# Where the operands of w_out begin in SBUF, and idle products around the second small turn, in a gated short-convolution layer on one Trainium2 core

## The chip, the cores and the metric

The kernel runs on one core of a Trainium2 chip. The metric is the device time of one execution in microseconds. The time before is the median of three runs, 915.63 us (915.52 to 916.85). One more execution was profiled; the rows quoted below are of that one.

## The reference

One layer is run (DEPTH is 1, so the recurrent mixer of the reference is never reached). Everything is float32.

```python
h = rmsnorm(x, norm_g)                                  # x: 256 tokens x 2048
shift, scale, gate = split(silu(c) @ ada_w + ada_b, 3)  # ada_w: 2048 x 6144
h = h * (1 + scale) + shift
b, cg, v, g = split(h @ w_in, 4)                        # w_in: 2048 x 16384
u = causal_conv3(cg * v)                                # per channel, 4096 channels
y = b * u * silu(g)                                     # 256 x 4096
x = x + gate * (y @ w_out)                              # w_out: 4096 x 2048
return rmsnorm(x, final_g)
```

## The kernel before

A float32 product is made of three products of a faster type: each operand is cast to `fp32r` ("hi"), the rest that the cast lost is the second operand ("lo"), and hi*hi, hi*lo and lo*hi are summed in PSUM. In the profile these are matmuls of 128 rows by 128 columns of weights with 256 or 512 columns of the moving operand.

**The order of the work.** The first some 26 us (lines 179 to 390) prepare. ScalarE's queue loads `rows1` (c, norm_g, ada_b), SyncE's queue loads x, the first slices of ada_w (`at0`) and of w_in. TensorE turns 16 rows of `rows1` for silu(c) ("the first small turn", line 243), turns the other 64 rows into `tp_v` ("the second small turn", line 246), and then makes `IDLE` = 6 idle products (`idle`, line 236), whose results nobody reads: a 128 x 128 float32 weight `ident` against a broadcast column of `ones`, 512 columns, each of them two records in the profile. Then x is turned, four 128-wide slices at a time (`turn_x`, line 284), with the sums of ada_w for shift and scale between (`sum0`, line 355: TensorE takes the slices k in `ON_PE`, VectorE the others at lines 377 and 379, and a product with `ones` adds VectorE's part, line 381). The order of this part is written out by hand: `in_order()` pins each engine's instructions to the order of the text.

Up to about 381 us the first half of w_in runs (`mm_s`, `part`, line 476) in an order that `plan()` makes, because shift and scale arrive piece by piece; then the second half up to about 731 us (`mm_b`, line 605). In both the slices of w_in are the stationary operand, 128 columns at a time, and the turned tokens `hT` are the moving operand, 256 columns (tokens) (`product`, line 447). From 731 us w_out runs, in four column blocks `dc` of 512 (line 771). Here it is the other way round: y (the layer's middle result, 128 tokens) is stationary, and hi or lo of a slice of w_out, 512 columns, is moving (`out_mm`, line 659). In blocks 0 and 1 the slices `ep` 5, 6 and 7, in block 2 the slices 5 and 6, are done by `seven` (line 689), a Strassen-like scheme on products of 256 columns: 42 products for each slice, whose stationary operands are y or sums of y (`form`, `form_g`, `form_h`). The slices come in the order 0, 1, 2, 5, 3, 6, 4, 7. Where nothing is pinned, a simulating scheduler sets the order within each engine.

**Buffers.** Each slice of weights is loaded into `raw` (SyncE's queue), ScalarE casts it to `hi` (line 321), VectorE subtracts to `lo` (line 326). All three kinds are 8 KB per partition and come from one pool, `wpool`, with three buffers each for the tags `raw`, `hi` and `lo`. In w_out the roles of two tags are exchanged: the slice is loaded into the tag `lo`, and the lo part goes to the tag `raw`. In the last block each loaded slice is first multiplied by the gate (line 796). A buffer is used again when its last reader is done, so a cast to `hi` waits for the products that read that buffer three slices before, and a load waits for VectorE.

**Where the buffers begin.** A pool puts its tiles one behind the other. Small unused tiles (`line`, `line0`, `line2`, `line3`, `line4`) shift what follows them. As the pools of this kernel lay the tiles out, these are the first bytes modulo 256 of what the products read:

| operand | in w_in | in w_out, before | in w_out, changed |
| --- | --- | --- | --- |
| moving | hT: 0 | hi and lo: 64 | hi and lo: 0 |
| stationary | hi: 64, lo: 192 | y, form, form_g: 128; form_h: 0 | y, form, form_g: 64; form_h: 0 |

Every slice that a product takes from such a tile is a multiple of 256 bytes further, so that all products of one row of the table have the same remainder.

Of the kernel before, what the change touches and what calls it, by code (L numbers as in the profile page):

```python
# [13 lines left out]
P = 128  # L14
# [103 lines left out]
def short_conv_layer(ctx: ExitStack, tc: tile.TileContext, x, c, norm_g, ada_w, ada_b, w_in, conv_w, w_out, final_g, out):  # L118
# [5 lines left out]
    line = ctx.enter_context(tc.tile_pool(name="line", bufs=1, side="right"))  # L124
    line.tile([P, 56], F32, tag="line", name="line")
    const = ctx.enter_context(tc.tile_pool(name="const", bufs=1))
    const.tile([P, 32], F32, tag="line0", name="line0")
    adap = ctx.enter_context(tc.tile_pool(name="adap", bufs=2))
    wpool = ctx.enter_context(tc.tile_pool(name="wpool", bufs=2))
    psum = ctx.enter_context(tc.tile_pool(name="psum", bufs=3, space=PSUM))  # L130
    hpool = ctx.enter_context(tc.tile_pool(name="hpool", bufs=1, side="right"))
    line2 = ctx.enter_context(tc.tile_pool(name="line2", bufs=1, side="right"))
    line2.tile([P, 32], F32, tag="line2", name="line2")
    slots = ctx.enter_context(tc.tile_pool(name="slots", bufs=NSLOT, side="right"))

    def slot(shape, name, dtype=F32):
        return slots.tile(shape, dtype, tag="slot", name=name)

    def raw_tile(name):
        return wpool.tile([P, SLOT], F32, tag="raw", name=name, bufs=3)  # L140

    after = mybir.DependencyInfo(mybir.DependencyClass.NoSync, mybir.DependencyReason.DATA)

# [37 lines left out]
    pinned.enter_context(in_order())  # L181


    rows1 = const.tile([80, P], F32, tag="rows1", name="rows1")
    rows2 = const.tile([96, P], F32, tag="rows2", name="rows2")
    HX = D // 2
    GIVE = 300
    LEAD = 80
    IDLE = 6
    ON_PE = (3, 7, 10, 11, 13, 15)  # L190
    xt = [[slot([P, HX], f"x{t}{dh}") for dh in range(2)] for t in range(TT)]
    nc.scalar.dma_start(rows1[64:80, :], c.rearrange("o (k p) -> (o k) p", p=P))
# [8 lines left out]
    adas = ada_w[0].rearrange("(k p) (s f) -> p k s f", p=P, s=3)  # L201
    NK0 = ADA[0]
    first_ada = []
    wpool.tile([P, 16], F32, tag="line4", name="line4", bufs=1)
    for n, (j, kk) in enumerate(((0, 4), (4, 4), (8, 4), (12, 2), (14, 1), (15, 1))):
        at = wpool.tile([P, SLOT], F32, tag=("lo", "hi")[n % 2], name="at0", bufs=3)[:, : kk * 2 * NK0 * P]
        at = at.rearrange("p (k s f) -> p k s f", k=kk, s=2)
        if n == 0:
            wpool.tile([P, 32], F32, tag="line3", name="line3", bufs=1)
        for s in range(2):  # L210
            nc.sync.dma_start(at[:, :, s, :], adas[:, j : j + kk, s, 0 : NK0 * P])
        first_ada.extend(at[:, i] for i in range(kk))
# [3 lines left out]

    ident = const.tile([P, P], F32, tag="ident", name="ident")
    make_identity(nc, ident)
    ones = const.tile([P, P], F32, tag="ones", name="ones")
    nc.vector.memset(ones, 1.0)  # L220
    eps_t = const.tile([P, 1], F32, tag="eps", name="eps_t")
    nc.vector.memset(eps_t, EPS)
# [5 lines left out]
    def turn(rows, lo, n, dst):  # L228
        tp = psum.tile([P, 512], F32, tag="sm", name="tp_v", bufs=2)[:, : n - lo]
        nc.tensor.transpose(tp, rows[lo:n, :], ident[lo:n, lo:n])  # L230
        if dst is not None:
            nc.vector.tensor_copy(dst, tp)
        return tp


    def idle(n):
        for _ in range(n):
            nc.tensor.matmul(tp_idle, ident, ones[:, 0:1].to_broadcast([P, 512]), start=True, stop=True)  # L238
# [4 lines left out]
    silu = nc.scalar.activation(silu_c, turn(rows1, 64, 80, None), AF.Silu)  # L243
    root = nc.scalar.activation(warm, eps_t, AF.Sqrt)
    tc.add_manual_dep(root.ins, silu.ins.name, after, reason="one change of table")
    tp_v = turn(rows1, 0, 64, None)
    gT = vec[:, 0:KT]
    bias = vec[:, KT : 3 * KT].rearrange("p (s k) -> p s k", s=2)
    idle(IDLE)


    ssq = const.tile([P, 2, TT], F32, tag="ssq", name="ssq")
# [57 lines left out]
            )  # L310
            nc.vector.tensor_tensor(out=hl_[k], in0=hf, in1=hh_[k].bitcast(F32), op=ALU.subtract)

    def hi_tile():
        return wpool.tile([P, SLOT], F32R, tag="hi", name="hi", bufs=3)

    def lo_tile(lo_tag="lo"):
        return wpool.tile([P, SLOT], F32R, tag=lo_tag, name="lo", bufs=3)

    def split_hi(raw, n, hi=None):
        hi = hi_tile() if hi is None else hi  # L320
# [17 lines left out]
        other_half[0] = tiles if n <= HALF else None  # L338
        return tiles

    def split(raw, n, lo_tag="lo"):

        return split_lo(raw, n, split_hi(raw, n), lo_tag)

# [174 lines left out]
    for kind, *step in plan():  # L521
        if kind == "ada":
            ada_piece(*step)
        else:
            ch, k1 = step[0], step[3]
            part(*step)
            if step[2] == 0 and len(acc) in LATER:
                with tc.issue_after(last_mm[0].ins), behind(ended):
                    if len(acc) == LATER[0]:
                        nc.sync.dma_start(rows2[:, :], conv_w.rearrange("w (k p) -> (w k) p", p=P))  # L530
                    else:
                        turn(rows2, 0, 96, cw)
            whole[ch] += k1 == KT
            if k1 == KT and whole[ch] == 4:
                mixed(ch)
# [26 lines left out]
    def gate_sums(dc, j, at3):  # L562
        nc.sync.dma_start(at3, adas[:, j : j + 2, 2, dc * 512 : (dc + 1) * 512])
        if j == 0:
            gacc[0] = adap.tile([P, 512], F32, tag="gv", name="gacc")
        ga = gacc[0]
        for i in range(2):
            s = silu_c[:, j + i : j + i + 1]
            if j + i == 0:
                nc.vector.tensor_scalar_mul(ga, at3[:, i, :], s)  # L570
            else:
                nc.vector.scalar_tensor_tensor(out=ga, in0=at3[:, i, :], scalar=s, in1=ga, op0=ALU.mult, op1=ALU.add)  # L572
        if j + 2 == KT:
            ps = psum.tile([P, 512], F32, tag="sm", name="ps_gate", bufs=2)
            nc.tensor.matmul(ps, ones, ga, start=True, stop=True)  # L575
            nc.vector.tensor_tensor(out=gate(dc), in0=ps, in1=gate(dc), op=ALU.add)

    KP = 8
# [110 lines left out]
    def seven(po, ps, ep, raw):  # L689


        opens = ep == SEVEN[0]
        if opens:
            first_of.clear()
        b = blocks(raw)
        sums = wpool.tile([P, SLOT], F32, tag="lo", name="sums_o", bufs=3)
        s = blocks(sums)
        nc.vector.tensor_tensor(
            out=s[:, :, 0:2], in0=b[:, :, 1:3], in1=b[:, :, 0:1].to_broadcast([P, 2, 2, NB]), op=ALU.subtract
        )  # L700
        hi, lo = hi_tile(), lo_tile("raw")
        bh, bl = blocks(hi), blocks(lo)
        nc.scalar.copy(bh[:, :, 1:4], b[:, :, 1:4])
        nc.vector.tensor_tensor(out=s[:, :, 2], in0=b[:, :, 2], in1=s[:, :, 0], op=ALU.add)
        nc.vector.tensor_tensor(out=s[:, :, 3], in0=b[:, :, 3], in1=s[:, :, 2], op=ALU.subtract)
        nc.vector.tensor_tensor(out=bl[:, :, 1:4], in0=b[:, :, 1:4], in1=bh[:, :, 1:4].bitcast(F32), op=ALU.subtract)
        sh, sl = (blocks(v) for v in split(sums, SLOT, "raw"))

        def y(pair, k, t):
            return [ys[pair][:, k, h, t * P : (t + 1) * P] for h in range(2)]  # L710

        def f(pair, j):
            return [forms[pair][h][:, j] for h in range(2)]

        left, right = slice(0, NB), slice(NB, 2 * NB)
        for r in range(2):
            pair = ep * 2 + r
            for dst, bank, form, j in (
                (ps[:, 1, left], 1, y(pair, 0, 0), 1),
                (po[0][:, right], None, y(pair, 1, 0), 3),  # L720
                (po[0][:, left], None, f(pair, 3), 2),
            ):
                seven_mm(dst, bank, opens and r == 0 and bank is not None, form, bh[:, r, j], bl[:, r, j])
        for r in range(2):
            pair = ep * 2 + r
            for dst, bank, form, j in (
                (ps[:, 0, left], 0, f(pair, 2), 1),
                (ps[:, 0, right], 0, f(pair, 0), 0),
                (ps[:, 1, right], 1, f(pair, 1), 2),
                (po[1][:, right], None, y(pair, 1, 1), 3),  # L730
            ):
                seven_mm(dst, bank, opens and r == 0 and bank is not None, form, sh[:, r, j], sl[:, r, j])
# [38 lines left out]
    for dc in range(4):  # L771
# [13 lines left out]
        for ep in orders[dc]:  # L785

            first = dc == 0 and ep == 0
            raw = wpool.tile([P, SLOT], F32, tag="raw" if first else "lo", name="raw_o", bufs=3)
            nc.sync.dma_start(
                raw.rearrange("p (k f) -> p k f", k=EP),  # L790
                w_out[0, ep * EP * P : (ep + 1) * EP * P, dcs].rearrange("(k p) f -> p k f", p=P),
            )
            if dc == 3:

                raw3 = raw.rearrange("p (k f) -> p k f", k=EP)
                nc.vector.tensor_tensor(  # L796
                    out=raw3, in0=raw3, in1=gate(dc).unsqueeze(1).to_broadcast([P, EP, 512]), op=ALU.mult
                )
            if dc == 0:
                load_ends(orders[dc].index(ep) - 3)  # L800
            if ep in sevens[dc]:
                seven(po, ps, ep, raw)
                continue
            hi, lo = split(raw, SLOT, "raw")
            out_mm(po[0], 0, ep, hi, lo)
            if dc == 3 and ep >= n_ep - LATE:
                late.append((ep, hi, lo))
            else:
                out_mm(po[1], 1, ep, hi, lo)
# [52 lines left out]
```

## Time and profile before

| | |
| --- | --- |
| median of three runs | 915.63 us |
| the profiled execution: its time, its span | 916.7 us, 914.6 us |
| preparation, up to the first product of w_in | 0 to 26.5 us |
| w_in, first half (`mm_s`), second half (`mm_b`) | 26.5 to 381 us, 381 to 731 us |
| w_out: first product, last product begins | 730.9 us, 905 us |
| busy in 731 to 848 us: TensorE, VectorE, ScalarE | 116.99, 94.61, 57.67 us of 117 |

The rows are read like this. A row of the timeline has the start in us, the busy time in us, the engine, the line, the operation, what is written <- what is read, the shapes, the count of merged instructions, and in brackets how long the engine was idle before and what ended that. "PE" is TensorE's matmul, "PEld" its load of a stationary operand, which overlaps matmuls; "DVE" is VectorE, "ACT" ScalarE, "SP" SyncE, which issues most DMAs. The duration of one matmul has its latency in it, and consecutive ones overlap: the pace is read from start to start. A row of the chain of waits has start, length, and what the end of the program hung on in that time, with the count of instructions.

### The profile page before, as it was taken

To read this page: it belongs to the slowest core of one execution; us is meant where nothing else is said; L and a number is where in the kernel's file an instruction comes from. 1 tells how busy PE (TensorE), PEld (TensorE's weight loads), DVE (VectorE), ACT (ScalarE), POOL (GpSimd) and SP (SyncE) were. 2 spreads that over 40 slices of the span, in tenths; PEclk is the share of its full clock that TensorE was granted. 3 is DMA by queue.
4 is the path that set the end of the run, shared out by engine and by line. 5 is a ranking of instruction groups with operands and counts; after the bars stand their busy time and mean duration, and the time that the engine had idled before them with its cause. 6 is when DMAs were issued, how large, how long until landed. Compare 5 with 4: busy or idle time off the path is not lost.

```text
span 914.6 us, 16626 instructions
## 1 busy us (share of the span) xinstructions
PE 897.3 (98%) x7191; PEld 862.6 (94%) x7191; DVE 665.3 (73%) x673; ACT 480.6 (53%) x430; POOL 0.7 (0%) x6
## 2 busy tenths in 40 slices
PE   6999999999999999999999999999999999999996
PEld 4999999999999999999999999999999988888884
DVE  4889899989888886765545776555555567888992
ACT  6868856665558756743344434344434445455442
POOL 0000000000000000000000000000000000000000
PEclk9999999999999999999999999999999999999998
DMA  9999999999998686675566787566666477465642
GB/s 311 370 371 347 360 315 352 358 369 362 328 330 273 201 285 194 197 249 190 185 194 199 257 272 230 185 188 198 199 199 185 141 282 250 156 229 170 244 139 92
DMA packets 163753, 227.66 MB, mean 249 GB/s; under 512 B 5680, under 2 KB 104160, under 8 KB 163296
## 3 DMA queue, kind: packets, MB, share of 16 engines
q1 hardware_dynamic: 163552, 226.56, 74.9%
q8 instruction: 56, 0.92, 0.4%
q14 instruction: 17, 0.14, 0.0%
q10 hardware_dynamic: 128, 0.04, 0.0%
HBM read 224.49 MB, written 2.10 MB: 248 GB/s over the span
## 4 chain that ended last, share of the span: by engine, by line
PE 97%; ACT 1%; DMA 1%; ACTq 0%; issue 0%; DVE 0%
PE mm_b L451 38%; PE mm_s L451 38%; PE mm_o L667 4%; PE mm_o L669 4%; PE mm_o L668 4%; PE mm L680 3%; PE mm_o L680 2%; PE tp_idle L238 1%; PE mm_l L667 1%; DMA rows<-in_ada_b_dram 1%; PE mm_l L668 1%; PE mm_l L669 1%; PE sum L360 1%; PE ps_gate L575 0%; PE tp_g L441 0%; PE tp_x L290 0%
## 5 line engine op out<-in xcount | busy, mean ns | idle before, releaser
L451 PE MATMUL mm_s<-hT,hi 128*128 128x256 f32 x2048 | 350.4, 277 | 0.1
L451 PE MATMUL mm_b<-hT,hi 128*128 128x256 f32 x2048 | 349.4, 276 | 0.0
L451 PEld LDWEIGHTS mm_s<-hT,hi 128*128 128x128 f32 x2048 | 308.5, 188 | 1.0 <-ACT hT L307 0.3
L451 PEld LDWEIGHTS mm_b<-hT,hi 128*128 128x128 f32 x2048 | 308.4, 188 | 0.5 <-issue 0.5
L451 PE MATMUL mm_b<-hT,lo 128*128 128x256 f32 x1024 | 282.6, 276 | 0.0
L451 PE MATMUL mm_s<-hT,lo 128*128 128x256 f32 x1024 | 282.2, 277 | 0.0
L326 DVE TENSOR_TENSOR lo<-raw,hi 128x2048 fp32r<-128x2048 f32 (+1 forms) x66 | 148.0, 2243 | 114.2 <-ACT hi L321 113.8
L321 ACT CAST hi<-raw 128x2048 fp32r<-128x2048 f32 (+1 forms) x66 | 123.7, 1874 | 192.7 <-PE mm_b L451 149.1
L451 PEld LDWEIGHTS mm_b<-hT,lo 128*128 128x128 f32 x1024 | 192.2, 188 | 0.5 <-issue 0.5
L451 PEld LDWEIGHTS mm_s<-hT,lo 128*128 128x128 f32 x1024 | 191.8, 188 | 0.3
L326 DVE TENSOR_TENSOR lo<-raw_s,hi 128x2048 fp32r<-128x2048 f32 (+1 forms) x80 | 147.6, 1850 | 34.6 <-ACT hi L321 33.6
L321 ACT CAST hi<-raw_s 128x2048 fp32r<-128x2048 f32 (+1 forms) x80 | 123.9, 1558 | 69.9 <-PE mm_s L451 60.5
L434 DVE SCALAR_TENSOR_TENSOR gv<-at,silu_c,gv 128x512 f32<-128x512 f32 x105 | 78.6, 749 | 3.6 <-DMA at<-in_ada_w_dram 1.8
L472 ACT COPY acc<-mm_s 128x1024 f32<-128x1024 f32 x54 | 54.7, 1014 | 37.7 <-PE mm_s L451 37.6
L321 ACT CAST hi<-raw_o 128x2048 fp32r<-128x2048 f32 x24 | 45.8, 1909 | 48.8 <-DVE raw_o L796 23.9
L326 DVE TENSOR_TENSOR lo<-raw_o,hi 128x2048 fp32r<-128x2048 f32 x24 | 54.9, 2290 | 12.5 <-ACT hi L321 12.2
L667 PE MATMUL mm_o<-hi,y 128*128 128x512 f32 x160 | 63.4, 396 | 0.0
L669 PE MATMUL mm_o<-hi,y 128*128 128x512 f32 x160 | 63.3, 395 | 0.0
L668 PE MATMUL mm_o<-lo,y 128*128 128x512 f32 x160 | 63.3, 395 | 0.0
L572 DVE SCALAR_TENSOR_TENSOR gacc<-at_g,silu_c,gacc 128x512 f32<-128x512 f32 x60 | 44.9, 749 | 6.0 <-DMA at_g<-in_ada_w_dram 4.9
L484 ACT COPY mm_s<-acc 128x1024 f32<-128x1024 f32 x38 | 38.5, 1017 | 0.7
L668 PEld LDWEIGHTS mm_o<-lo,y 128*128 128x128 f32 x160 | 30.1, 188 | 7.0
(152 smaller groups left out, 635.0 us busy)
## 6 DMA issues: line engine op xcount, KB each, us to landing
raw<-in_sc_w_in_dram SPq DMA_DIRECT2D x64, 1024.0 KB, 5.7
raw_s<-in_sc_w_in_dram SPq DMA_DIRECT2D x47, 1024.0 KB, 7.7
raw_o<-in_sc_w_out_dram SPq DMA_DIRECT2D x32, 1024.0 KB, 5.2
at<-in_ada_w_dram SPq DMA_DIRECT2D x114, 256.0 KB, 7.7
raw_s<-in_sc_w_in_dram SPq DMA_DIRECT2D x33, 512.0 KB, 7.0
at_g<-in_ada_w_dram SPq DMA_DIRECT2D x32, 512.0 KB, 8.0
at<-in_ada_w_dram SPq DMA_DIRECT2D x6, 512.0 KB, 9.3
x<-in_x_dram SPq DMA_DIRECT2D x4, 512.0 KB, 6.2
```

The lines of the kernel that those rows point to most:

```text
L238: nc.tensor.matmul(tp_idle, ident, ones[:, 0:1].to_broadcast([P, 512]), start=True, stop=True)
L321: nc.scalar.copy(hi[:, :n], raw[:, :n])
L326: nc.vector.tensor_tensor(out=lo[:, :n], in0=raw[:, :n], in1=hi[:, :n].bitcast(F32), op=ALU.subtract)
L434: nc.vector.scalar_tensor_tensor(out=gv, in0=at4[:, i], scalar=c_k, in1=gv, op0=ALU.mult, op1=ALU.add)
L451: mm = last_mm[0] = nc.tensor.matmul(dst, w, h[k], start=begins and left, stop=ends, skip_group_check=True)
L472: nc.scalar.copy(acc[ch, q], bank)
L484: nc.scalar.copy(bank, acc[ch, q])
L572: nc.vector.scalar_tensor_tensor(out=ga, in0=at3[:, i, :], scalar=s, in1=ga, op0=ALU.mult, op1=ALU.add)
L667: nc.tensor.matmul(po, yh, hi[:, o], start=opens, stop=False, skip_group_check=True)
L668: nc.tensor.matmul(po, yh, lo[:, o], start=False, stop=False, skip_group_check=True)
L669: nc.tensor.matmul(po, yl, hi[:, o], start=False, stop=ct == NCT - 1, skip_group_check=True)
L680: mm = nc.tensor.matmul(dst, form[a], b, start=opens and i == 0 and bank not in first_of, stop=False, skip_group_check=True)
```

## The change

It has two parts.

**Places.** Small tiles are added or made larger (`line0` 48, `line1` 24, `line2` 48 words, `line3` to `line6`); the nine buffers of `wpool` become nine tags of one buffer each (`w_tile`), taken in turn as before, and are laid out lo, lo, lo, then hi and raw alternately. A `hi` buffer is 48 words (192 bytes) longer, and in w_out the hi part begins at word 48 (`SIDE`) of it, in w_in at word 0 as before. So w_in's operands begin where they did, and those of w_out where the table above says. `rows1` and `rows2` now share one buffer, and `ones` has one column instead of 128, which line 575 reads as a broadcast.

**Idle products.** There are eight instead of six: three before the second small turn, five behind it.

```diff
-    const.tile([P, 32], F32, tag="line0", name="line0")
+    const.tile([P, 48], F32, tag="line0", name="line0")
     adap = ctx.enter_context(tc.tile_pool(name="adap", bufs=2))
+    adap.tile([P, 24], F32, tag="line1", name="line1", bufs=1)
...
-    line2.tile([P, 32], F32, tag="line2", name="line2")
+    line2.tile([P, 48], F32, tag="line2", name="line2")
...
+    SIDE = 48
+    nth = {"raw": 0, "hi": 0, "lo": 0}
+    def pad(n, name, pool=wpool):
+        pool.tile([P, n], F32, tag=name, name=name, bufs=1)
+    def w_tile(kind, name, dtype=F32, i=None):
+        if i is None:
+            i = nth[kind] % 3
+            nth[kind] += 1
+        return wpool.tile([P, SLOT + SIDE * (kind == "hi")], dtype, tag=f"{kind}{i}", name=name, bufs=1)
+    pad(32, "line4")
+    for i in range(3):
+        w_tile("lo", "place", i=i)
+    pad(32, "line3")
+    for i in range(3):
+        w_tile("hi", "place", i=i)
+        w_tile("raw", "place", i=i)
+        if i < 2:
+            pad(16, f"line{5 + i}")
...
-    rows1 = const.tile([80, P], F32, tag="rows1", name="rows1")
-    rows2 = const.tile([96, P], F32, tag="rows2", name="rows2")
+    def rows_tile(name):
+        return const.tile([96, P], F32, tag="rows", name=name)
+    rows1 = rows_tile("rows1")
...
-    IDLE = 6
+    IDLE = (3, 5)
...
-    ones = const.tile([P, P], F32, tag="ones", name="ones")
+    ones = const.tile([P, 1], F32, tag="ones", name="ones")
...
+    idle(IDLE[0])
     tp_v = turn(rows1, 0, 64, None)
...
-    idle(IDLE)
+    idle(IDLE[1])
...
-    def hi_tile():
-        return wpool.tile([P, SLOT], F32R, tag="hi", name="hi", bufs=3)
+    def hi_tile(c0=0):
+        return w_tile("hi", "hi", F32R)[:, c0 : c0 + SLOT]
...
-        hi, lo = hi_tile(), lo_tile("raw")
+        hi, lo = hi_tile(SIDE), lo_tile("raw")
...
-        sh, sl = (blocks(v) for v in split(sums, SLOT, "raw"))
+        sh, sl = (blocks(v) for v in split(sums, SLOT, "raw", hi_tile(SIDE)))
...
-            hi, lo = split(raw, SLOT, "raw")
+            hi, lo = split(raw, SLOT, "raw", hi_tile(SIDE))
```

How this moves instructions on TensorE at the program's start: `tp_v` is what the two small turns write (16 and 64 columns), `tp_idle` what the idle products write, and `tp_x` the turned x. Before:

```order
L230 MATMUL tp_v<-ident,rows_82 128x16
L230 MATMUL tp_v<-ident,rows_82 128x64
L238 MATMUL tp_idle<-ones,ident 128x512 x6
L290 MATMUL tp_x<-ident,x_84 128x128
L290 MATMUL tp_x<-ident,x_86 128x128
```

With the change (the lines of the text are 23 to 24 further down):

```order
L253 MATMUL tp_v<-ident,rows_96 128x16
L261 MATMUL tp_idle<-ones,ident 128x512 x3
L253 MATMUL tp_v<-ident,rows_96 128x64
L261 MATMUL tp_idle<-ones,ident 128x512 x5
L314 MATMUL tp_x<-ident,x_97 128x128
L314 MATMUL tp_x<-ident,x_99 128x128
```

Three idle products now stand where nothing stood between the two turns, and five where there were six. From there up to the first product of w_in the order on TensorE is as before; in w_in groups of turns for shift and scale move by a few products.

In w_out, TensorE's order is the same but for a few products within one slice of `seven`. This is the first slice of that kind (block 0, slice 5), where the second half of its products begins; `mm_8251` and `mm_8265` are the bank that `seven` sums in, y_4456 and y_4470 the same y. Before:

```order
L680 MATMUL mm_8251<-hi,form 128x256
L680 MATMUL mm_8251<-lo,form 128x256
L680 MATMUL mm_8251<-hi,form 128x256 x2
L680 MATMUL mm_8251<-lo,form 128x256
L680 MATMUL mm_8251<-hi,form 128x256 x2
L680 MATMUL mm_8251<-lo,form 128x256
L680 MATMUL mm_8251<-hi,form 128x256
L680 MATMUL mm_o<-hi,y_4456 128x256
```

With the change:

```order
L705 MATMUL mm_8265<-hi,form 128x256
L705 MATMUL mm_o<-hi,y_4470 128x256
L705 MATMUL mm_8265<-lo,form 128x256
L705 MATMUL mm_8265<-hi,form 128x256 x2
L705 MATMUL mm_8265<-lo,form 128x256
L705 MATMUL mm_8265<-hi,form 128x256 x2
L705 MATMUL mm_8265<-lo,form 128x256
L705 MATMUL mm_8265<-hi,form 128x256
```

The first product with y moves ahead of the first that reads `lo`, as it already stands in the later slices of that kind before the change.

More of the change, by code (lines that the diff above doesn't have):

```diff
@@ L137, in slot @@
         return slots.tile(shape, dtype, tag="slot", name=name)
+    SIDE = 48
[16 more added lines that the diff above has]
+            pad(16, f"line{5 + i}")
     def raw_tile(name):
-        return wpool.tile([P, SLOT], F32, tag="raw", name=name, bufs=3)
+        return w_tile("raw", name)
     after = mybir.DependencyInfo(mybir.DependencyClass.NoSync, mybir.DependencyReason.DATA)
@@ L203, in short_conv_layer @@
     first_ada = []
-    wpool.tile([P, 16], F32, tag="line4", name="line4", bufs=1)
     for n, (j, kk) in enumerate(((0, 4), (4, 4), (8, 4), (12, 2), (14, 1), (15, 1))):
-        at = wpool.tile([P, SLOT], F32, tag=("lo", "hi")[n % 2], name="at0", bufs=3)[:, : kk * 2 * NK0 * P]
+        at = w_tile(("lo", "hi")[n % 2], "at0")[:, : kk * 2 * NK0 * P]
         at = at.rearrange("p (k s f) -> p k s f", k=kk, s=2)
-        if n == 0:
-            wpool.tile([P, 32], F32, tag="line3", name="line3", bufs=1)
         for s in range(2):
@@ L311, in modulate @@
             nc.vector.tensor_tensor(out=hl_[k], in0=hf, in1=hh_[k].bitcast(F32), op=ALU.subtract)
-    def hi_tile():
-        return wpool.tile([P, SLOT], F32R, tag="hi", name="hi", bufs=3)
+    def hi_tile(c0=0):
+        return w_tile("hi", "hi", F32R)[:, c0 : c0 + SLOT]
     def lo_tile(lo_tag="lo"):
-        return wpool.tile([P, SLOT], F32R, tag=lo_tag, name="lo", bufs=3)
+        return w_tile(lo_tag, "lo", F32R)
     def split_hi(raw, n, hi=None):
@@ L339, in places, with split @@
         return tiles
-    def split(raw, n, lo_tag="lo"):
-        return split_lo(raw, n, split_hi(raw, n), lo_tag)
+    def split(raw, n, lo_tag="lo", hi=None):
+        return split_lo(raw, n, split_hi(raw, n, hi), lo_tag)
     sums0 = psum.tile([P, 512], F32, tag="sm", name="sum0", bufs=2)
@@ L529, in short_conv_layer @@
                     if len(acc) == LATER[0]:
+                        rows2 = rows_tile("rows2")
                         nc.sync.dma_start(rows2[:, :], conv_w.rearrange("w (k p) -> (w k) p", p=P))
@@ L574, in gate_sums @@
             ps = psum.tile([P, 512], F32, tag="sm", name="ps_gate", bufs=2)
-            nc.tensor.matmul(ps, ones, ga, start=True, stop=True)
+            nc.tensor.matmul(ps, ones.to_broadcast([P, P]), ga, start=True, stop=True)
             nc.vector.tensor_tensor(out=gate(dc), in0=ps, in1=gate(dc), op=ALU.add)
@@ L695, in seven @@
         b = blocks(raw)
-        sums = wpool.tile([P, SLOT], F32, tag="lo", name="sums_o", bufs=3)
+        sums = w_tile("lo", "sums_o")
         s = blocks(sums)
@@ L787, in short_conv_layer @@
             first = dc == 0 and ep == 0
-            raw = wpool.tile([P, SLOT], F32, tag="raw" if first else "lo", name="raw_o", bufs=3)
+            raw = w_tile("raw" if first else "lo", "raw_o")
             nc.sync.dma_start(
```

## The prediction

> **What bounds the kernel now.** The page first: what is busy, and on what the end hangs.
>
> ```profile
> span 914.6 us, 16626 instructions
> PE 897.3 (98%) x7191; PEld 862.6 (94%) x7191; DVE 665.3 (73%) x673; ACT 480.6 (53%) x430; POOL 0.7 (0%) x6
> ...
> PE 97%; ACT 1%; DMA 1%; ACTq 0%; issue 0%; DVE 0%
> ```
>
> TensorE bounds it: 97% of the chain. But busy is not at peak, so I read the pace. The chain of waits in order of time, for w_in and for the 256-column products of w_out:
>
> ```profile
> 542.89 43.56 PE mm_b L451 x384
> 587.31 143.75 PE mm_b L451 x1268
> ...
> 749.98 1.06 PE mm L680 x9
> ...
> 762.10 1.02 PE mm L680 x9
> ```
>
> In w_in a product of 256 columns takes 143.75 / 1268 = 113.4 ns (43.56 / 384 the same, although that stretch begins just behind other products). In `seven` the same size takes 117.8 ns in one group of nine and 113.3 in another, with the same operands' positions: two paces, 4.4 ns apart. The timeline of TensorE for 512 columns, late in block 3, where ScalarE and VectorE are idle (36 starts lie between the first and the last row):
>
> ```profile
> 763.30 0.39 PE L667 MATMUL mm_o<-hi,y 128*128 128x512 f32 x1
> 763.52 0.28 PE L680 MATMUL mm<-hi,y 128*128 128x256 f32 x1
> ...
> 893.62 0.40 PE L669 MATMUL mm_l<-hi,y 128*128 128x512 f32 x1
> 893.85 0.39 PE L667 MATMUL mm_l<-hi,y 128*128 128x512 f32 x1
> 894.09 0.40 PE L668 MATMUL mm_l<-lo,y 128*128 128x512 f32 x1
> ...
> 902.02 0.40 PE L669 MATMUL mm_o<-hi,y 128*128 128x512 f32 x1
> ```
>
> (902.02 - 893.62) / 36 = 233.3 ns, alternately 0.23 and 0.24. Twice w_in's pace would be 226.7. The upper two rows show one product that does run so: 0.22 us to the next start, right behind a group at 113.3. So w_out pays about 6.7 ns more for 512 columns and 4.4 for 256 than w_in's pace. No neighbour causes it: the pace is the same with ScalarE and VectorE idle.
>
> **The change part by part: the places in w_out.** How many products there are, from the groups by line (the lines 668 and 669 have the same counts):
>
> ```profile
> L667 PE MATMUL mm_o<-hi,y 128*128 128x512 f32 x160 | 63.4, 396 | 0.0
> L667 PE MATMUL mm_l<-hi,y 128*128 128x512 f32 x32 | 12.7, 396 | 0.0
> ```
>
> 3 x 192 = 576 of 512 columns; `seven` is called 8 times with 42 products, 336 of 256 columns. Whether the new places bring w_in's pace no row of before can show: no product there has moving at 0 and only stationary at 64. The bounds: below, nothing, since the moving operand and the stationary one stay 64 bytes apart as before (64 and 128, then 0 and 64), and if only the distance counts nothing changes; above, w_in's pace for all. I take w_in's pace: it has just these two positions for two of every three products (hi; the third, lo, is at 192), and behind the gate's products at 542.89 it is at a mean of 113.4 again, where w_out holds either pace for whole groups. If all of it showed, it would be 576 x 6.7 = 3.8 us, and about three quarters of the 336 (the rest stand in groups at 113.3) at 4.4 = 1.1 us: 4.9 us.
>
> Not all shows. In block 0, from slice 5's cast on, ScalarE and VectorE are the chain:
>
> ```profile
> 747.93 1.91 ACT L321 CAST hi<-raw_o 128x2048 fp32r<-128x2048 f32 x1 [3.69 <-PE mm_o L669]
> 749.87 2.29 DVE L326 TENSOR_TENSOR lo<-raw_o,hi 128x2048 fp32r<-128x2048 f32 x1 [3.31 <-ACT hi L321]
> ...
> 756.41 1.91 ACT L321 CAST hi<-sums_o 128x2048 fp32r<-128x2048 f32 x1 [4.88 <-DVE sums_o L705]
> 758.35 2.29 DVE L326 TENSOR_TENSOR lo<-sums_o,hi 128x2048 fp32r<-128x2048 f32 x1 [2.05 <-ACT hi L321]
> ...
> 760.47 0.28 PE L680 MATMUL mm_o<-hi,y 128*128 128x256 f32 x1
> 760.70 0.38 PE L680 MATMUL mm<-lo,form 128*128 128x256 f32 x1
> ...
> 769.03 2.29 DVE L326 TENSOR_TENSOR lo<-sums_o,hi 128x2048 fp32r<-128x2048 f32 x1 [2.05 <-ACT hi L321]
> ...
> 771.75 0.28 PE L680 MATMUL mm<-lo,form_g 128*128 128x256 f32 x1
> ```
>
> The cast at 747.93 waits for TensorE to give up a buffer; from there cast, subtraction, sums, cast, subtraction follow without a pause on both engines, and TensorE's first product with `lo` starts 0.06 us after the subtraction ends (758.35 + 2.29 = 760.64, start 760.70), and again at 771.75 (771.32). TensorE waits there already (760.47 to 760.70 is two products' time). What TensorE gains between 747.7 and 771.7 becomes more of this wait. Block 1 has the same order and length of work, block 2 has one such slice behind its first: by block 0's 24.0 and 13.0 us, 24 + 24 + 13 = 61 us in which the pace gains nothing. In them lie 5 slices of 24 products of 512 columns, 120 x 6.7 = 0.8 us, and nearly all of the 256-column gain; 456 x 6.7 = 3.1 us remain. In block 3 VectorE is close as well:
>
> ```profile
> 853.00:903.00 50.00, 50.00 (x216) 40.28 (x215) 40.67 (x31) 16.62 (x12) 0.00 (x0) 1.00 0.39 134
> ...
> 889.18 4.49 DVE L326 TENSOR_TENSOR lo<-raw_o,hi 128x2048 fp32r<-128x2048 f32 x2
> ```
>
> It works without a pause from 853 to 893.67, but then TensorE has 11 us of products left, of which 24 need the last `lo`; a TensorE that is 1.2 us earlier there still finds it. **This part: -3.1 us**, between 0 and -4.9.
>
> **The idle products.** The timeline of the preparation:
>
> ```profile
> 4.06 0.25 PE L230 MATMUL tp_v<-ident,rows 16*128 16x16 f32 x1 [4.06 <-DMA rows<-in_c_dram]
> 8.49 0.34 PE L230 MATMUL tp_v<-ident,rows 64*128 64x64 f32 x1 [4.18 <-DMA rows<-in_ada_b_dram]
> 8.76 8.39 PE L238 MATMUL tp_idle<-ones,ident 128*128 128x512 f32 x12
> ...
> 12.51 4.27 ACT L351 ACTIVATE x<-x,rstd 128x1024 f32<-128x1024 f32 x4 [0.23 <-DVE rstd L269]
> 14.04 0.34 PEld L238 LDWEIGHTS tp_idle<-ones,ident 128*128 128x128 f32 x1 [0.52 <-issue]
> 14.83 0.19 PEld L238 LDWEIGHTS tp_idle<-ones,ident 128*128 128x128 f32 x1 [0.45 <-issue]
> 15.26 0.19 PEld L238 LDWEIGHTS tp_idle<-ones,ident 128*128 128x128 f32 x1 [0.24 <-issue]
> 16.98 1.91 PE L290 MATMUL tp_x<-ident,x 128*128 128x128 f32 x16
> ...
> 19.33 3.63 DVE L379 SCALAR_TENSOR_TENSOR gv<-at,silu_c,gv 128x512 f32<-128x512 f32 x5 [0.69 <-DMA at<-in_ada_w_dram]
> ...
> 24.52 1.05 PE L360 MATMUL sum<-ones,gv 128*128 128x128 f32 x8
> 26.52 0.74 PE L451 MATMUL mm_s<-hT,hi 128*128 128x256 f32 x4
> ...
> 33.02 1.06 ACT L321 CAST hi<-raw_s 128x1024 fp32r<-128x1024 f32 x1 [0.87 <-DMA raw_s<-in_sc_w_in_dram]
> ```
>
> A record of an idle product takes 0.85 us at first and 0.43 from about 14.8: the clock rises 6 us after TensorE began steady work at 8.76. The turn of x waits for them until 16.98, although its inputs, two of the four operations at 12.51, are there at 14.65. With the change three idle products start at 4.35, where TensorE waits for a DMA until 8.4 anyway: if the clock again takes 6 us, it rises at 10.4, after (6.0 - 0.3) / 0.85 = 6.7 of the 16 records; the other 9.3 take 4.0 us, to 14.4. The turns then start at 14.65, 2.3 us earlier. VectorE holds them up later: its five sums end at 19.33 + 3.63 = 22.96, and they wait for a DMA; the product with `ones`, now at 24.52, can come 1.5 us earlier and w_in with it. If the clock rises no earlier than now, 4.2 of the 16 records are left at 14.8, the end is at 16.6, and the gain 0.4. Behind that, w_in's slices come by DMA: ScalarE waits for one at 33.02, so some of the 1.5 us may be lost. Bounds 0 and -1.5; I take **-1.0**, nearer the upper, since later in w_in TensorE waits for nothing.
>
> The Trainium skill, "TensorE: Matmul & The Clock Gate", Part 1, says that the clock rises after a busy window of 3.4 us that runs freely: 3.4 to 6.8 us after work begins. The 6 us of this trace lie within that, and the idle products would end between 13.3 and 14.8 by an estimate from it.
>
> Nothing else costs: `ones` as a broadcast is read by four products `ps_gate`; the shared rows buffer is free long before conv_w is loaded.
>
> **The sum.** -3.1 - 1.0 = -4.1 us, from the profiled execution's 916.7 (span 914.6 and 2.1 around it) 912.6. That execution lies 1.1 above the median of the runs, 915.63; from the median: **911.5 us**.
>
> **The rivals.** *Places make no difference* (only the distance counts, or the pace is w_out's own): for it speaks the same distance, and that one place holds both paces; against it that w_in always settles. Only the idle products stay: 914.6.
>
> The same skill page, Part 2, has TensorE read both operands through two independent ports, so that a load of weights takes nothing from a running matmul, and gives a gap of 215.8 ns for 512 columns. The 233.3 here disagrees with the figure; by the rule of the ports the places are indifferent, and the time that of this rival.
>
> *The new places collide more*: the steps seen are some 4.5 ns; if w_out goes up one instead of down, 912 products x 4.5 = +4.1, less 1.0: 918.7. It decides against the change from (1.0 + 1.83) / 912 = 3.1 ns per product on. For it speaks that nothing shows how moving at 0 behaves with stationary at 64 alone.
>
> *All of it shows*: VectorE's chain shifts with TensorE, and the idle products give 1.5: -4.9 - 1.5, 909.2. Against it stand the two starts right behind a subtraction.
>
> That the operands don't lie where the change says is excluded by the layout, except `form_h`, which stays at 0 (24 products).
>
> **How the numbers follow.** Forecast 0.60 (909.5 to 913.5), all of it 0.06, no difference 0.22, collision 0.12. What a measurement can tell from no change is 0.2%, 1.83 us: under 913.8 is faster. The forecast and "all" give faster 0.66; "no difference" and a small part of the others same 0.24; collision slower 0.10. The range, 908.5 to 915.6, takes in "all" and "no difference" and leaves out the collision.
>
> **What would show it.** Right: late in block 3 starts 227 ns apart without alternation, all groups of `seven` at 113.3, longer waits before the first product with `lo` in blocks 0 and 1, the first product of w_in at about 25.0. Wrong: 233 ns as before (places indifferent), or 236 and more (collision); `tp_x` still near 17 (the clock rises late); a wait of TensorE within 26 to 60 us that eats the start.

## The result, and the profile after

The changed kernel takes 916.15 us (median of 14 runs, 915.83 to 916.97), the kernel before 915.83 (14 runs, 915.28 to 916.85): ratio 1.0003, 95% interval 0.9995 to 1.0011. Nothing was gained; 911.5 us had been forecast. The profiled execution took 916.3 us.

The page of the changed kernel: its span, what is busy, and the shares of the chain that ended last.

```profile
span 914.1 us, 16641 instructions
PE 899.7 (98%) x7195; PEld 863.3 (94%) x7195; DVE 664.6 (73%) x673; ACT 480.4 (53%) x430; POOL 0.7 (0%) x6
...
PE 91%; ACT 3%; DMA 2%; DVE 2%; issue 1%; SPq 0%; ACTq 0%
```

TensorE is as busy as before, but six hundredths of the chain have moved from it to ScalarE, DMA and VectorE: at a few short waits, of some tenths of a us each, the chain now leaves it. Its pace in block 3 (timeline, starts in the first column; 36 starts lie between the first and the last row):

```profile
887.78 0.39 PE L693 MATMUL mm_l<-lo,y 128*128 128x512 f32 x1
888.02 0.40 PE L694 MATMUL mm_l<-hi,y 128*128 128x512 f32 x1
888.25 0.39 PE L692 MATMUL mm_o<-hi,y 128*128 128x512 f32 x1
...
896.18 0.39 PE L692 MATMUL mm_o<-hi,y 128*128 128x512 f32 x1
```

(896.18 - 887.78) / 36 = 233.3 ns, in steps of 0.23 and 0.24: exactly the pace before. The new places brought nothing in the 512-column products. In `seven` both paces stand beside each other, as they did before (chain; groups of nine at 113.3 and 117.8 ns):

```profile
761.49 1.02 PE mm L705 x9
...
793.78 1.06 PE mm L705 x9
```

The timeline of the preparation:

```profile
4.14 0.25 PE L253 MATMUL tp_v<-ident,rows 16*128 16x16 f32 x1 [4.14 <-DMA rows<-in_c_dram]
4.33 5.49 PE L261 MATMUL tp_idle<-ones,ident 128*128 128x512 f32 x6
9.75 0.37 PE L253 MATMUL tp_v<-ident,rows 64*128 64x64 f32 x1
10.04 4.62 PE L261 MATMUL tp_idle<-ones,ident 128*128 128x512 f32 x10
14.50 0.27 PE L314 MATMUL tp_x<-ident,x 128*128 128x128 f32 x1
15.12 1.86 PE L314 MATMUL tp_x<-ident,x 128*128 128x128 f32 x15 [0.35 <-ACT x L375]
...
25.34 0.74 PE L475 MATMUL mm_s<-hT,hi 128*128 128x256 f32 x4 [0.33 <-ACT hT L331]
```

The six slow records take 5.49 us, the ten behind the turn 4.62, so the clock is up from about 10; the turn of x begins at 14.50 and waits for its input only, and w_in starts at 25.34 instead of 26.52. This half of the mechanism came as forecast. But the second half of w_in shows little of it (chain, start and length):

```profile
380.49 160.93 PE mm_b L475 x1420
542.28 43.55 PE mm_b L475 x384
586.68 143.74 PE mm_b L475 x1268
```

380.49 stands against 381.10 before: of 1.18 us, 0.61 are left. The waits of TensorE's weight loads between 24 and 110 us name where the rest went (us in total, times, longest); in the profile of before, the row with VectorE's `lo` and that with `hi` are not there, and `hT` is 0.3:

```profile
PEld mm_s L475 <- ACT hT L331: 0.6, 1, 0.6
PEld mm_s L475 <- DVE lo L350: 0.4, 1, 0.4
PEld mm_s L475 <- ACT hi L345: 0.3, 1, 0.3
```

### The profile page after: what moved, and what is told of

It reads as the page before. It is cut to its first block, busy times and chain, and to the rows that moved or that the text cites. A ratio compares the mean times of both kernels' runs of the same rounds, so it can differ in the third digit from the quotient of the medians.

```text
span 914.1 us, 16641 instructions
## 1 busy us (share of the span) xinstructions
PE 899.7 (98%) x7195; PEld 863.3 (94%) x7195; DVE 664.6 (73%) x673; ACT 480.4 (53%) x430; POOL 0.7 (0%) x6
## 4 chain that ended last, share of the span: by engine, by line
PE 91%; ACT 3%; DMA 2%; DVE 2%; issue 1%; SPq 0%; ACTq 0%
PE mm_b L475 38%; PE mm_s L475 37%; PE mm_o L692 4%; PE mm_o L694 4%; PE mm_o L693 4%; PE mm L705 2%; ACT hi L345 1%; PE mm_o L705 1%; DMA at<-in_ada_w_dram 1%; PE mm_l L692 1%; PE mm_l L694 1%; PE mm_l L693 1%; DVE lo L350 1%; DMA x<-in_x_dram 1%; DMA raw<-in_sc_w_in_dram 1%
```

## The experiments

### Bare groups: every pair of places

A kernel without the layer, of groups of 48 products (`REPEAT`), with nothing beside them; per place one buffer, begun 16 words further each:

```diff
+        for r in range(4):
+            t = pool.tile([P, D + 64], F32R, tag=f"{kind}{r}", name=f"{kind}_{'abcd'[r]}")
+            v = t[:, 16 * r : 16 * r + D]
...
+            tiles[kind, r] = v
...
+        for k in range(REPEAT):
+            j = k // 3 % 4
+            m = tiles["ml" if k % 3 == 1 else "mh", mr][:, j * 512 : j * 512 + n]
+            w = tiles["st", srs[k % len(srs)]][:, k % 16 * P : (k % 16 + 1) * P]
+            mm(ps[:, 0:n], w, m, k == 0, k == REPEAT - 1)
```

> Leaves out the whole layer: it writes x to the output and runs groups of 48 products, with nothing else on the core, one group for each pair of places: the moving operand (m) and the stationary operand (s) begin at a = 0, b = 64, c = 128 or d = 192 modulo 256, in 512 columns (wide) and 256 (slim); two more groups per moving place take the stationary operands in the order b, b, d as w_in does. Theory 1, only the distance moving minus stationary counts: all groups of one distance have one pace, and those at distance 192 (w_out before and after) show 233.3 ns wide and 113.3 or 117.8 slim; another distance shows 226.7. Theory 2, the pace is the product's own and places don't matter: all 16 wide groups at 233.3, slim ones at 113.3 or 117.8 at random. Theory 3, each place counts by itself: wide m a with s b (w_out after) differs from m b with s c (w_out before). Theory 4, the order b, b, d holds the low pace: the groups with b, b, d at 113.3 and 226.7, those with b alone at 117.8 and 233.3.

Two groups of 512 columns in the timeline: the second product and the last (46 starts between them).

```profile
24.07 0.39 PE L44 MATMUL wide_ma_sb<-ml_a,st_b 128*128 128x512 f32 x1
...
34.79 0.40 PE L44 MATMUL wide_ma_sb<-mh_a,st_b 128*128 128x512 f32 x1
...
69.29 0.40 PE L44 MATMUL wide_mb_sb<-ml_b,st_b 128*128 128x512 f32 x1
...
79.76 0.39 PE L44 MATMUL wide_mb_sb<-mh_b,st_b 128*128 128x512 f32 x1
```

10.72 / 46 = 233.0 ns with moving at 0 and stationary at 64 (w_out as changed), 10.47 / 46 = 227.6 with both at 64. The chain of the same kernel has whole groups (start, length; the length holds a constant start and end as well):

```profile
80.36 11.20 PE wide_mb_sc L44 x48
...
125.76 10.92 PE wide_mc_sc L44 x48
...
136.90 11.20 PE wide_mc_sd L44 x48
...
199.45 5.46 PE slim_ma_sb L44 x48
...
222.79 5.76 PE slim_mb_sb L44 x48
...
252.22 5.76 PE slim_mc_sc L44 x48
258.20 5.66 PE slim_mc_sd L44 x48
```

The mean of the last 30 steps from start to start in each group, ordered by the distance, moving minus stationary modulo 256:

| distance | 512 columns, ns (four groups) | 256 columns, ns (four groups) |
| --- | --- | --- |
| 0 | 226.7 each | 120.0 each |
| 64 | 228.9 each | 117.8 three times, 113.3 once |
| 128 | 232.2 to 232.7 | 118.7 three times, 120.0 once |
| 192 | 233.3 each | 113.3 three times, 117.8 once |

For 512 columns theory 1 holds, and where both begin doesn't count: mb_sc (w_out before) and ma_sb (w_out after) have one distance, 192, and one pace. For 512 columns it is the worst of the four; distance 0, which neither kernel has there, is the best. For 256 columns it is nearly the other way round, and at 64 and 192 a group falls into one of two paces; with one group for each pair of places these groups don't tell what decides between the two. Theory 4 is not borne out here: of the groups in the order b, b, d, slim with moving at 0 (w_in's own places) is at 113.3, but so is the group with b alone, where theory 4 asks for 117.8. The other slim ones are at 118.2 to 119.1, and the wide ones at 231.1 to 233.3, not 226.7.

### Bare groups: the second of three products at another place

```diff
-            m = tiles["ml" if k % 3 == 1 else "mh", mr][:, j * 512 : j * 512 + n]
+            m = (tiles["ml", lr] if k % 3 == 1 else tiles["mh", mr])[:, j * 512 : j * 512 + n]
```

> Leaves out the whole layer, as the run named bench1; the stationary operand is at 64 in every group, and of each three products the first and third have the moving operand at one place (the outer two letters after m), the second at another (the letter between), all 16 pairs for 512 columns and for 256. Theory 1, with each product's pace set by its own distance and that of its neighbours: groups with one distance as in bench1 (wide 233.3, 226.7, 228.9, 232.2 for a, b, c, d), mixed ones near the weighted mean, and 256 columns with distances 192, 64, 192 (maca) settle at 113.3 as w_in does. Theory 2: no order among the groups.

The groups with one distance repeat the table, but for 512 columns at distance 128, which are 0.6 ns above it: 512 columns at 226.7 (distance 0), 228.9, 233.3 (128 and 192), 256 columns at 120.0, 117.8, 118.7, 113.3. The mixed ones of 512 columns lie at 228.9 to 234.5, so a mixture never comes below the best pure one. The case forecast to settle at 113.3 (maca) did not: 117.8. So distances of the moving operand mixed so don't do what w_in's mixed stationary places do; why is open.

### The two parts alone

The places alone, with six idle products as before (the edit below), and the idle products alone: three and five of them in the kernel before, whose places stay.

```diff
-    IDLE = (3, 5)
+    IDLE = (0, 6)
```

> The places alone: the changed kernel with all six idle products behind the second small turn as before the change. Theory A (the places make no difference, the idle products bring what is left of 1 us): within 0.5 us of the kernel before, w_out's 512-column products at 233 ns. Theory B (the new places cost something, which eats the gain of the idle products): 0.5 to 1.5 us slower than before, with longer stretches of TensorE in w_in or w_out than before.

916.08 us against 915.83 (ratio 1.0, interval 0.9991 to 1.0009); 512 columns at 233 again: by the times, theory A. The one profile of it has something of theory B too: from w_out's first product to the start of its last it is 175.33 us, where the three profiles of the kernel before have 174.26 to 174.38, and the weight loads' waits between 728 and 900 us are 1.9 us instead of 0.5 to 0.8.

> The idle products alone: the kernel before with three idle products ahead of the second small turn and five behind it. Theory A: the first product of w_in at about 25.3 us and 0.3 to 1.2 us faster than before. Theory B (the earlier start is lost in w_in): first product of w_in at 25.3, the second half of w_in no earlier than before by 0.3 us, the time within 0.3 us of before.

916.12 us against 915.83 (ratio 1.0005, interval 0.9997 to 1.0014). In its profile w_in starts at 25.09 (before 26.52), the second half at 380.46 (before 381.10). Neither theory fits whole: 0.64 of 1.43 us are left at 380 us, and in the times nothing.

### w_in with all products at one distance

```diff
-    pad(32, "line4")
+    pad(64, "line4")
...
-    pad(32, "line3")
```

> The changed kernel with the lo buffers of w_in at 64 instead of 192, so that every product of w_in has the moving operand at 0 and the stationary one at 64, as w_out in the changed kernel. Theory 1 or 4 (the third product at another place makes w_in settle at 113.3): w_in's products go to 117.8 for part or all of the time, 5 to 27 us slower (6144 products x 4.4 ns = 27). Theory 2 (the places are indifferent): w_in at 113.3, within 1 us of the changed kernel.

921.08 us, ratio to before 1.0061 (interval 1.0047 to 1.0075): 5.25 us slower than the kernel before and 4.9 slower than the changed kernel's 916.15, at the lower end of the 5 to 27 us of theories 1 and 4. Its chain, first in this kernel and then in the changed one:

```profile
168.30 30.86 PE mm_s L474 x262
199.96 33.33 PE mm_s L474 x283
...
544.40 45.22 PE mm_b L474 x384
590.48 143.73 PE mm_b L474 x1268
```

```profile
168.46 29.73 PE mm_s L475 x262
198.99 32.13 PE mm_s L475 x283
```

30.86 / 262 and 45.22 / 384 are 117.8 ns, where the changed kernel has 113.4 in the same stretches; others stay at 113.4. So in w_in too, moving at 0 with stationary at 64 holds either pace. What makes w_in settle at the lower one in these stretches is the third product's other place, 192, and not these two places themselves.

### w_out's 512-column products at distance 0

The lo buffers of w_out become 16 words longer and begin at 64, and the hi part begins at word 0, which is 64 too; the two small pads between these buffers go, and `seven` keeps its places.

```diff
-        return wpool.tile([P, SLOT + SIDE * (kind == "hi")], dtype, ...)
+        return wpool.tile([P, SLOT + SIDE * (kind == "hi") + MORE * (kind == "raw")], dtype, ...)
...
-            hi, lo = split(raw, SLOT, "raw", hi_tile(SIDE))
+            hi, lo = split_lo(raw, SLOT, split_hi(raw, SLOT, hi_tile(0)), lo=lo_tile("raw", 16))
```

> The changed kernel with the moving operand of the 512-column products of w_out at 64, where y is (distance 0 instead of 192); the 256-column products of w_out keep moving 0 and stationary 64. Theory 1 (the pace is set by the distance moving minus stationary alone, 226.7 ns at 0 and 233.3 at 192 for 512 columns): w_out's 512-column products at 226.7 without alternation, and 456 x 6.6 ns = 3.0 us faster than the changed kernel, 2.5 to 3.8, since 120 of the 576 lie where ScalarE and VectorE hold TensorE. Theory 2 (w_out's pace comes from something else in w_out, its PSUM banks or its buffers, that the bare groups lack): 233 as before and no difference beyond 0.7 us.

913.24 us, ratio to before 0.9972 (interval 0.9961 to 0.9983): 2.5 us faster than the kernel before, 2.9 than the changed kernel's 916.15, as theory 1 has it. Its block 3, again 36 starts:

```profile
887.76 0.39 PE L691 MATMUL mm_o<-lo,y 128*128 128x512 f32 x1
887.98 0.39 PE L692 MATMUL mm_o<-hi,y 128*128 128x512 f32 x1
...
895.92 0.39 PE L691 MATMUL mm_l<-lo,y 128*128 128x512 f32 x1
```

8.16 / 36 = 226.7 ns, the pace the prediction had hoped for, at the distance that the change did not set. From w_out's first product to the start of its last it is 902.04 - 730.08 = 171.96 us; in the changed kernel 904.82 - 730.26 = 174.56. That is 2.6 us where 576 x 6.6 = 3.8 would be in all (all four profiles with the 512 columns at distance 0 have 171.8 to 172.0 us there, all seven with distance 192 have 174.3 to 175.3). Where the rest is shows in the chain of this kernel in block 0:

```profile
746.65 1.92 ACT hi L343
...
757.10 2.17 issue
759.28 2.30 DVE lo L348
761.59 6.53 DMA raw_o<-in_sc_w_out_dram
768.22 1.92 ACT hi L343
```

The chain leaves TensorE for ScalarE's casts and VectorE's subtractions, here and again at 789 and 832 us, and here also for a load that waited for its buffer until the subtraction ended; in the changed kernel it leaves only at 747 and 833 us. The weight loads of this kernel wait 1.7 us for VectorE and ScalarE between 728 and 900 us (the two rows below), those of the changed kernel 0.9.

> As the run named near, and the 256-column products of w_out are moved to distance 0 too (moving and stationary at 64). Theory 1: 512 columns at 226.7, 256 columns in w_out at 120.0 instead of 113.3 to 117.8, so slower than near by up to 336 x 5 ns = 1.7 us, of which five slices of eight lie where ScalarE and VectorE hold TensorE: 0.3 to 1.0 us slower than near. Theory 2: no difference from the changed kernel.

913.30 us (913.04 to 913.71), with the 256-column products at 120 ns: not slower than 913.24. The forecast 0.3 to 1.0 us did not come. The waits of weight loads between 728 and 900 us, in near and then in nearall, say where the extra time goes: into waits for VectorE and ScalarE that become shorter or go.

```profile
PEld mm L703 <- DVE lo L348: 1.1, 3, 0.6
PEld mm_o L690 <- ACT hi L343: 0.6, 2, 0.4
```

```profile
PEld mm L703 <- DVE lo L348: 0.4, 1, 0.4
```

### When the clock rises

The kernel before, profiled twice more, and the version at distance 0 with six idle products:

> The kernel before once more, for a second profile. Theory A (the moment at which the clock rises differs from one execution to the next, and the profiled execution of before had a late one): the first product of w_in anywhere from 25.0 to 26.6 us, the clock rising 4 to 6.3 us after the idle products begin. Theory B (it is fixed): the first product at 26.5 again, the last idle product ending at 17.0.

> The kernel before, a third profile. Theory A: the clock may rise anywhere from 3.9 to 6.8 us after the idle products begin, and the first product of w_in starts between 25.2 and 26.6 us. Theory B (before always has the late rise, places was an exception of its own): 6.0 us and 26.2 to 26.5 us again.

> As the run named near, with the six idle products behind the second small turn, as before the change. Theory A (the moment at which the clock rises differs from one execution to the next, 3.9 to 6.1 us after the idle products begin in the profiles so far, so that six idle products reach w_in sometimes earlier and sometimes later than three and five do): within 0.5 us of near, 912.7 to 913.7. Theory B (the three and five bring about 1 us): 913.9 to 914.5. The other way round, if the early start costs something in w_in: 912.0 to 912.7.

The twelve records of the idle products and the first product of w_in, in the third profile of the kernel before, and the idle products in the run of the places alone:

```profile
8.59 7.57 PE L238 MATMUL tp_idle<-ones,ident 128*128 128x512 f32 x12
...
25.53 0.73 PE L451 MATMUL mm_s<-hT,hi 128*128 128x256 f32 x4
```

```profile
8.54 7.31 PE L261 MATMUL tp_idle<-ones,ident 128*128 128x512 f32 x12
```

The same twelve records took 8.39 us in the profile on which the prediction rests, 8.36 in the second, and 7.57 and 7.31 here. Counting the slow records, the clock rose 3.8 to 6.0 us after the idle products began: theory A, which the third profile shows; the second, with w_in at 26.22, came out almost like the first. For the kernel before the whole time follows it: starts of w_in at 26.52, 26.22 and 25.53 us go with 916.7, 916.27 and 915.65 us. In the run of the places alone it doesn't: w_in starts at 25.23, and the profiled execution takes 916.38 us, with the longer w_out named above. The version with six idle products took 913.33 us (912.27 to 913.69), against 913.24 with three and five: theory A, no difference.

### ScalarE's order at the start of w_in

The scheduler's order on ScalarE depends on the count of idle products. With six, the first cast of a `raw_s` stands ahead of the last four operations `xs`; with three and five it stands behind them, and they take 1.5 us. One run puts the first order back, with three and five:

```diff
+        n_kept = len(nc.cur_bb.bb.instructions)
         keep_x(3, tp_3)
+        kept = list(nc.cur_bb.bb.instructions[n_kept:])
...
+                while kept:
+                    tc.add_manual_dep(kept.pop(), nc.cur_bb.bb.instructions[-1].name, after, reason="behind")
```

> As the run named near (three and five idle products), but on ScalarE the last four operations that keep the turned x (xs, the fourth group) are put behind the first cast of w_in's next slice (raw_s), as they stand with six idle products; with three and five the scheduler puts them ahead of it. Theory A (this order on ScalarE is what eats the earlier start of w_in: in six profiles of six idle products the second half of w_in begins 354.5 to 354.7 us after the first product, in three of three and five 355.1 to 355.4): first product of w_in at about 25.0, the second half begins 354.5 to 354.8 us after it, at 379.6 to 379.9 instead of 380.3, and 0.3 to 0.7 us faster than near, 912.5 to 912.9. Theory B (the early start is lost to the loads of w_in, whatever ScalarE's order): 355.1 to 355.4 us as before and the time of near, 912.9 to 913.6.

912.97 us (912.35 to 913.79), ratio to before 0.9968 (interval 0.9956 to 0.998), which can't be told from 913.24. The waits of the weight loads between 24 and 110 us:

```profile
PEld mm_s L475 <- ACT hT L329: 0.6, 1, 0.6
PEld mm_s L475 <- ACT mm_s L508: 0.3, 1, 0.3
PEld mm_s L475 <- ACT hi L343: 0.2, 1, 0.2
```

In the version with three and five (near), the weight loads wait for VectorE's `lo` at 27.4 us and for `hi` at 28.9, and the 31st product of w_in starts 4.48 us after the first; with six idle products, and here, it starts after 4.01. So the order explains these two waits, and 0.47 us, as theory A says. But the `hi` wait in the last row is another one, and the chain shows where it comes from:

```profile
36.70 0.40 ACT acc L496
...
37.62 2.00 ACT hi L343 x2
39.66 15.92 PE mm_s L475 x137
```

On ScalarE two casts now stand behind a copy `acc` that has waited for TensorE, and TensorE's weight load at 39.66 waits for the second of them. By the 151st product w_in is as late as in near, 18.1 us after its first product instead of 17.6 to 17.7, and the second half begins 380.10 - 24.98 = 355.12 us after the first product, not 354.5 to 354.8: the forecast of theory A did not come. The order at 25 us is what loses most of the time in near; with it put right, nearly the same is lost at the next place. The expectation counted one profile of six idle products too many: 354.53 to 354.67 are from five.

## Why the prediction was wrong

**What bounds the kernel** was read rightly: TensorE, at two paces some 4.5 ns (256 columns) and 6.7 ns (512) apart.

**The places, -3.1 us: this step failed**, and with the words "I take w_in's pace: it has just these two positions for two of every three products". It read the pace off the absolute places. The runs show that the distance sets it (for 256 columns it leaves two paces open at 64 and 192), and moving at 64 with 64 bytes between became moving at 0 with the same 64 between, so nothing changed, but for the 24 products with `form_h` (distance 64, then 0). The lower bound of that very step ("if only the distance counts nothing changes") was the right end. Two facts that the rows of before don't show plainly made the choice look better than it was. First, w_in's 113.4 ns belong to its third product's place: with that taken away, w_in falls back to 117.8 in part. Second, 512 columns are not twice 256: at distance 192 the larger product is at its slowest (233.3) while the smaller may be at its fastest (113.3). The rows of before that pointed to it were a group of `seven` at 113.3 at just w_out's places and 512 columns at the same places at 233: one distance, and each width with its own best.

**How much shows** was sized well, though it was applied to the wrong places: 3.1 of 3.8 us were to remain in the 512-column products, and 2.6 did when the pace really fell. That the gain of `seven` lies hidden in blocks 0 to 2 is borne out: 120 ns in nearly all its products costs nothing that can be measured.

**The idle products, -1.0 us: this step failed too.** The mechanism was right up to the first product of w_in (25.34; "about 25.0" was forecast), the gain was not there. Two things were mis-sized. The base: one profiled execution had a late clock, while the median of the runs, from which the sum was made, need not have it; that this execution was 1.1 us above the median was noted and not asked after. Over the profiles the second half of w_in begins at 379.87 to 381.10 us with six idle products (five profiles, mean 380.5), and at 380.10 to 380.49 with three and five (four, mean 380.3; the runs with another lo place and another ScalarE order left out). On the mean w_in starts 0.8 us earlier (25.9, then 25.1 us), not 1.5, and 0.6 of that is gone by 380 us. And the loss: "some of the 1.5 us may be lost" was taken as a third, and in these profiles 0.5 to 0.8 us are lost. That the edit would also turn ScalarE's order around at 25 us, which costs 0.47 us of this, was not looked at; the prediction looked at TensorE's order alone. What the unprofiled runs do at their start no profile shows.

The clock's moment, 3.8 to 6.0 us after the idle products begin, also lies within 3.4 to 6.8 us, the estimate that the prediction works out from the Trainium skill, "TensorE: Matmul & The Clock Gate", Part 1, which gives a busy window of some 3.4 us that runs freely. The prediction cited the rule and then took before's 6.0 us as its base, as if it were fixed; the range is what counts.

**The rivals.** "Places make no difference" is what happened, with its first reason (the distance); its 914.6 us was 1.5 too low, 1.0 of it the idle term. The same page of the Trainium skill, Part 2, has two independent ports for the two operands, and by the prediction's reading of that rule the places should not matter at all: for this change that gives the right answer, but not for the right reason, since 226.7 and 233.3 ns differ by the distance alone. "The new places collide more" did not happen, and could not at an unchanged distance.

## What to carry to other kernels

Before costing a change of buffer places for products like these, write down the difference between the two operands' starts for every product: if it doesn't change, expect nothing, and look for the best difference for each width separately (here 0 for 512 columns). Bare groups of products with nothing beside them find it in one run. Where a term rests on when the clock rises, profile the kernel before several times first, and after an edit at the start compare the order on all engines, not on the one edited.

## What the runs showed of the hardware that was not expected

- The pace of back-to-back fp32r products depends on the moving operand's start minus the stationary one's, modulo 256 bytes: 226.7, 228.9, 232.2 to 233.3 and 233.3 ns for 512 columns at 0, 64, 128 and 192; for 256 columns 120.0 ns at 0, 118.7 (once 120.0) at 128 and, at 64 and 192, either 113.3 or 117.8. Only starts that are multiples of 64 were tried, and why the distance acts is not shown.
- A group stays at the one of two paces into which it fell. A third product at another stationary place makes w_in (6144 products) settle at the lower one; without it 5.25 us are lost. Why this mixture does it, and a mixture of moving places does not, is open.
- The version with 512 columns at distance 0 beats both kernels at 913.24, the kernel before by 2.5 us; its variants (256 columns at 0 too, six idle products, the other ScalarE order) lie at 912.97 to 913.33 and can't be told apart.
